# Two-layer trunk on one core: mem and its factors ahead of the memory keys, a stage between store and broadcast of the gate sums

## The chip, the core and the metric

The kernel runs on one core of a Trainium2 chip. The core has a matrix engine (TensorE, PE in the profile; its weight loads are PEld), a vector engine (VectorE, DVE), a scalar engine for activations (ScalarE, ACT), a general engine (GpSimd, POOL) and an engine that here only issues transfers (SyncE, SP). Each engine works through its own instructions; semaphores hold an instruction until its operands are there. The metric is the device time of one execution in microseconds. Before the change it is 629.26 us, the median of three runs (628.68 to 629.43).

## The reference

A trunk of two layers over 256 tokens of width 1024. Each layer has 12 self-attention heads (layer 0 with forget gates, layer 1 block-sparse with ALiBi) and 4 heads that attend to 256 fixed memory tokens, then a SwiGLU FFN. What the change touches is the memory path and the gates of layer 0:

```python
xn = rms_norm(h, norm_mix[i])
mn = rms_norm(mem, norm_mem[i])
mkv = mn @ w_mem_kv[i]                        # keys and values of the memory heads
...
log_f = jax.nn.log_sigmoid(f_logit + b_fgate[j])
F = jnp.cumsum(log_f, axis=-1)                # the gate sums
s = q @ k * scale + F[t] - F[s]               # causal, then softmax, then times v
mem_out = memory_attention(qm, mk, mv)        # softmax(qm mk / 8) mv
h = h + heads @ w_out[i]
h = h + (silu(gate) * up) @ w_down[i]
```

rms_norm divides a row by the root of its mean square. The kernel multiplies by the gain first and puts the factor per token (1 / root) in after the matmul.

## The kernel before

**Matmuls in three passes.** Every f32 operand is split in two rounded parts, hi and lo, and a product is three matmuls: hi by hi, lo by hi, hi by lo (`prod`). The split of a weight block of 128 x 1024 is one ACT instruction (hi, L204) and one DVE instruction (lo, L205).

**The weight stream.** All weights and the transposed inputs lie in one stream in the order of use, in units of up to 128 x 2048. SP loads unit after unit into `raw`, which has 4 buffers; a load waits until its buffer has been read. `weights(i, kk)` asks for a block; it splits up to 5 halves ahead (AHEAD) and loads 3 units ahead of the split (FETCH). Units that are not weights (xT, memT, mem) are only read raw. In the orders below `raw8` is unit 8 of the stream, `hi9_0` the first half of unit 9 after its split.

**What sets the order.** PE and SP keep the order in which the program is written; ACT, DVE and POOL get theirs from a scheduler when the kernel is built. On the chip every engine keeps its order.

**Layer 0 around the change.** PE computes values and gates (`v_ps`), then queries and keys of heads 0 to 3 (`qk_ps`, 96 matmuls), spreads the factors of x over the partitions (`rsb_ps_x`: a matmul with the identity; ACT copies it to `rsb_x`), and then runs `memory_heads`. That takes `mem_kv(0)` in stages: memT is multiplied with its gain and split (`split_x` into `xh_mem` and `xl_mem`, one ACT and one DVE instruction per 128 rows of memT, k = 0 to 7), and four stages of 24 matmuls give `mk_ps` and `mv_ps`, two of them from each of the two weight units (mkv). Between the stages `step()` advances the generators in `active`. Then come 48 matmuls for the memory queries (`qm_ps`), the scores of the first memory heads (`s_m`) among the 96 matmuls of heads 4 to 7, and so on.

**The factors of mem.** mem itself (not transposed) is loaded as a unit of its own; `factor` takes for each half of its tokens the mean square on ACT (`junk_mem`, L232), adds EPS on DVE (`me_mem`, L243) and takes the power -0.5 on POOL (`rs_mem`, L245). `spread` turns both `rs_mem` on PE (`rsb_ps_mem`), and ACT copies that to `rsb_mem`. The keys are multiplied with `rsb_mem` on DVE and split on ACT, DVE and POOL (`mk`, L358 to L361); the queries are split as `xqm` (L351, L353). Both must be there for `s_m`.

**The gate sums.** `gate_sums` is a generator in `active`. Its second step sums the gates on PE (`F_ps`), copies them (`fr`, DVE), stores them to memory (`fd`, L479), loads them back as a broadcast in three parts (`fk`, L482) and computes `Fq_ps` and `fq`. `bias` reads `fk` and `fq` for heads 0 and 1 at the scores after the first `s_m`.

Of the kernel before, what the change touches and what calls it, by code (L numbers as in the profile page):

```python
# [30 lines left out]
S = 256  # L31
NT = S // P
KD = D // P
# [45 lines left out]
class Plan:  # L79


    def __init__(self, a):
        self.shapes, self.blocks, self.U = [], [], {}
        U = self.U
        xT = np.ascontiguousarray(a["x"][0].T)
        memT = np.ascontiguousarray(a["mem"][0].T)
        U["xT"] = self.unit([xT], 0, KD, 0, S)
        for i in range(2):
            w = a["w_in_fox"][0] if i == 0 else a["w_in_moba"][0]
            nv = SW + (H if i == 0 else 0)  # L90
            U["vf", i] = []
            for u in range(4):
                U["vf", i].append(self.unit([w], 2 * u, 2, 2 * SW, nv))
            for g in range(3):
                if g == MEM_AT[i]:
                    if i == 0:
                        U["memT", 0] = self.unit([memT], 0, KD, 0, S)
                        self.mkv(a, 0)
                        self.blocks.append(a["mem"][0].reshape(NT, P, D).transpose(1, 0, 2).reshape(-1))
                        self.shapes.append((NT, 1, D))  # L100
                        U["mem"] = len(self.shapes) - 1
                    U["qm", i] = self.unit([w], 0, KD, 2 * SW + nv, MW)
                U["qk", i, g] = [self.unit([w[:, :SW], w[:, SW:]], 4 * u, 4, g * 2 * P, 2 * P) for u in range(2)]
            U["out", i] = [self.unit([a["w_out"][i]], 2 * j, 2, 0, D) for j in (3, 0, 1, 2)]
            U["gu", i], U["dn", i] = {}, {}
            wgu = a["w_gate_up"][i]
            for c in range(NFC + 1):
                if c < NFC:
                    U["gu", i][c] = [self.unit([wgu[:, :DFF], wgu[:, DFF:]], 4 * u, 4, c * FC, FC) for u in range(2)]
                if c > 0:  # L110
                    U["dn", i][c - 1] = self.unit([a["w_down"][i]], 2 * (c - 1), 2, 0, D)
            if i == 0:
                U["memT", 1] = self.unit([memT], 0, KD, 0, S)
                self.mkv(a, 1)
# [13 lines left out]
def trunk(ctx: ExitStack, tc: tile.TileContext, plan, stream, x, gains, norm_final, b_fgate, square, out):  # L128
# [28 lines left out]
    def bank(name):  # L157
        return Bank(pp.tile([P, 512], F32, tag="bank", name=name))
# [12 lines left out]
    U = plan.U  # L171
# [3 lines left out]
    ready, raws, counts = {}, {}, [0, 0]  # L175
    AHEAD, FETCH = 5, 3

    def fetch():
        i = counts[0]
        sh = plan.shapes[i]  # L180
        n = int(np.prod(sh))
        raw = wp.tile([P, UNIT], F32, tag="raw", name=f"raw{i}", bufs=4)
        raws[i] = raw[:, :n].rearrange("p (a b c) -> p a b c", a=sh[0], b=sh[1])
        src = stream[int(starts[i]):int(starts[i + 1])].rearrange("(p c) -> p c", p=P)
        cuts = {0: [0, n // 8, n // 4, n // 2, n], 1: [0, HEAD, n // 2, n], 2: [0, n // 2, n]}.get(i, [0, n])
        for c0, c1 in zip(cuts, cuts[1:]):
            yield lambda c0=c0, c1=c1: nc.sync.dma_start(raw[:, c0:c1], src[:, c0:c1])
        counts[0] += 1

    def fetch_to(n):  # L190
        while counts[0] < min(len(plan.shapes), n):
            for f in fetch():
                f()
# [17 lines left out]
    def weights(i, kk):  # L211

        while (i, kk) not in ready:
            split()
        while counts[1] < min(len(halves), ready[i, kk][2] + 1 + AHEAD):
            split()
        return ready[i, kk][:2]
# [11 lines left out]
    def mean_square(src, name):  # L229
        junk = ap.tile([P, D], BF16, tag="work", name=f"junk_{name}", bufs=WORK_BUFS)  # L230
        ms = sp.tile([P, 1], F32, tag="ms", name=f"ms_{name}")
        nc.scalar.activation(junk[:, :src.shape[-1]], src, AF.Square, scale=D ** -0.5, accum_out=ms)  # L232
        return ms

    def factor(src, name):

        ms = mean_square(src, name)
        return inverse_root(ms, EPS, name)

    def inverse_root(ms, more, name):  # L240

        me = sp.tile([P, 1], F32, tag="me", name=f"me_{name}")
        nc.vector.tensor_scalar_add(me, ms, more)  # L243
        rs = sp.tile([P, 1], F32, tag="rs", name=f"rs_{name}", bufs=8)
        nc.gpsimd.tensor_tensor(rs, me, minus_half, op=ALU.pow)  # L245
        return rs

    def spread(rs, name, scales, tag):

        b = bank(f"rsb_ps_{name}")  # L250
        for t in range(NT):
            b.mm(b.t[:, t * P:(t + 1) * P], rs[t].to_broadcast([P, P]), ident, stop=True)
        n = len(scales)
        r = ap.tile([P, n, S], F32, tag=f"rsb_{tag}", name=f"rsb_{name}", bufs=1)
        for j, v in enumerate(scales):
            nc.scalar.activation(r[:, j, :], b.t[:, :S], AF.Copy, scale=v)
        return r

    def xposed(name):
        xh = ap.tile([P, KD, S], F32R, tag="xh", name=f"xh_{name}", bufs=2)  # L260
        xl = ap.tile([P, KD, S], F32R, tag="xl", name=f"xl_{name}", bufs=2)
        return xh, xl
# [13 lines left out]
    def split_x(i, gain, dst, ks=range(KD)):  # L276

        fetch_to(i + 1)
        for k in ks:
            split_ps(dst[0][:, k, :], dst[1][:, k, :], raws[i][:, k, 0, :], gT[:, k, gain:gain + 1])  # L280
# [28 lines left out]
    rs_mem = []  # L309
    rsb_mem = []  # L310

    def mem_kv(i):

        xs = xposed(f"mem{i}")
        split_x(U["memT", i], 2 + i, xs, range(MEM_AHEAD))
        yield
        kb, vb = bank(f"mk_ps{i}"), bank(f"mv_ps{i}")
        for u in range(2):
            for kk in range(4):
                wh, wl = weights(U["mkv", i][u], kk)  # L320
                k = 4 * u + kk
                mv_ = (xs[0][:, k, :], xs[1][:, k, :])
                if k + MEM_AHEAD < KD:
                    split_x(U["memT", i], 2 + i, xs, (k + MEM_AHEAD,))
                for p in range(HM // 2):
                    c = slice(p * P, (p + 1) * P)
                    prod(kb, kb.t[:, p * S:(p + 1) * S], (wh[:, 0, c], wl[:, 0, c]), mv_, k == KD - 1)
                for t in range(NT):
                    c = slice(MW, 2 * MW)
                    prod(vb, vb.t[:, t * S:(t + 1) * S], tok(xs, k, t), (wh[:, 0, c], wl[:, 0, c]), k == KD - 1)  # L330
                if kk % 2:
                    yield
        if i == 0:
            fetch_to(U["mem"] + 1)
            rs_mem.extend(factor(raws[U["mem"]][:, t, 0], f"mem{t}") for t in range(NT))
            rsb_mem.append(spread(rs_mem, "mem", (1.0,), "mem")[:, 0, :])
        mk = ap.tile([P, HM // 2, S], F32, tag="work", name=f"mk{i}", bufs=WORK_BUFS)
        nc.vector.tensor_mul(mk, kb.t.rearrange("p (a s) -> p a s", a=2), rsb_mem[0].unsqueeze(1).to_broadcast([P, 2, S]))
        for p in range(HM // 2):
            split_keys(mks[p], mk[:, p])  # L340
        for t in range(NT):
            nc.scalar.activation(mvs[t][:, :, 0:DH], vb.t[:, t * S:(t + 1) * S].rearrange("p (a d) -> p a d", d=DH),
                                 AF.Copy, scale=rs_mem[t])
# [86 lines left out]
    def mixer(i, xs, rs):  # L430
# [41 lines left out]
        def gate_sums():  # L472
            yield
            fb = bank("F_ps")
            fb.mm(fb.t[:H, 0:S], lf[:, 0], prefix)
            fb.mm(fb.t[:H, P:S], lf[:, 1], prefix[:, 0:P], stop=True)
            fr = ap.tile([P, 2, S], F32, tag="work", name="fr", bufs=WORK_BUFS)[:H, 0]
            nc.vector.tensor_copy(fr, fb.t[:H, :S])
            nc.sync.dma_start(fd, fr)  # L479
            for g in range(GATE_PARTS):  # L480
                hs = slice(g * (H // GATE_PARTS), (g + 1) * (H // GATE_PARTS))
                nc.sync.dma_start(fk[:, hs], fd[hs].unsqueeze(0).to_broadcast([P, H // GATE_PARTS, S]))  # L482
            gb = bank("Fq_ps")
            for t in range(NT):
                for u in range(t + 1):
                    gb.mm(gb.t[:, t * H:(t + 1) * H], prefix[:, (t - u) * P:(t - u + 1) * P], lf[:, u], stop=u == t)
            nc.scalar.activation(fq.rearrange("p t h -> p (t h)"), gb.t[:, :NT * H], AF.Copy)
# [280 lines left out]
```

## Time and profile before

| | |
|---|---|
| median of three runs | 629.26 us |
| profiled execution, its own time | 630.81 us |
| its span | 629.0 us |
| PE busy | 611.8 us (97%) |
| PEld busy | 525.6 us (84%) |
| DVE busy | 399.9 us (64%) |
| ACT busy | 363.7 us (58%) |
| POOL busy | 60.2 us (10%) |
| mean rate of the transfers | 178 GB/s |

Durations come from the profiled execution; its own time is the span and 1.8 us around it. Busy matmuls overlap one another: back to back, two 256-column matmuls start 0.12 us apart, though one takes 0.28 us from its start to its end. A number in brackets in a timeline is the time that the engine stood idle ahead of the row, and who ended it. "PEclk" or the clock column is the granted clock of TensorE, where 1.00 is 2.4 GHz and 0.50 is 1.2 GHz.

### The profile page before, as it was taken

The page shows a single profiled execution, that of the slowest core. Times are in us where ns is not written, and L with a number is a line of the kernel's source. Part 1 is how long each engine was busy: PE and PEld are TensorE (multiplying, and loading weights), DVE is VectorE, ACT ScalarE, POOL GpSimd, SP SyncE. Part 2 cuts the span into 40 slices and gives each one's busy share as a digit, 9 for nine tenths or more (in the row PEclk, how much of TensorE's full clock was granted, in tenths as well). Part 3 has the DMA queues.
Part 4 walks back from the last instruction along what each step waited for, and adds up shares of the span by engine and source line. Part 5 has one row for each costly group of instructions (what it writes and reads, how often), then busy time and mean ns, then how long its engine had stood idle before and what let it go on. Part 6 is the DMA issues. An engine that isn't in the chain of part 4 may idle for free.

```text
span 629.0 us, 8916 instructions
## 1 busy us (share of the span) xinstructions
PE 611.8 (97%) x3364; PEld 525.6 (84%) x3364; DVE 399.9 (64%) x697; ACT 363.7 (58%) x646; POOL 60.2 (10%) x90
## 2 busy tenths in 40 slices
PE   7999899999999999999999999999999999999995
PEld 5999887778888888888899999877888888888884
DVE  4588899976455544457475589986644455445535
ACT  6679878666444444446376589876644444444423
POOL 2021344300000000000011033100000000000000
PEclk8999899999999999999999999999999999999999
DMA  8984822435554445545555533332455445555301
GB/s 289 367 315 166 338 74 103 151 143 201 202 196 168 178 194 201 179 173 207 193 185 198 216 144 114 133 135 83 160 193 200 178 172 190 198 200 198 136 2 67
DMA packets 17635, 112.27 MB, mean 178 GB/s; under 512 B 2220, under 2 KB 2744, under 8 KB 5432
## 3 DMA queue, kind: packets, MB, share of 16 engines
q1 hardware_dynamic: 17304, 111.42, 48.4%
q8 instruction: 26, 0.43, 0.3%
q10 hardware_dynamic: 288, 0.29, 0.1%
q14 instruction: 17, 0.14, 0.1%
HBM read 110.64 MB, written 1.06 MB: 178 GB/s over the span
## 4 chain that ended last, share of the span: by engine, by line
PE 84%; DVE 6%; ACT 5%; DMA 2%; issue 2%; POOL 0%; SPq 0%; POOLq 0%; ACTq 0%; DVEq 0%
PE gu L167 38%; PE d_acc L167 18%; PE qk_ps L167 9%; PE v_ps L167 6%; PE o_acc L167 5%; DMA raw<-in_stream 2%; DVE lo L205 2%; PE hT L628 2%; PE s_s L167 1%; ACT hi L204 1%; PE mv_ps L167 1%; PE qm_ps L167 1%; PE mk_ps L167 1%; ACT p_s L395 1%; PE s_m L167 1%
## 5 line engine op out<-in xcount | busy, mean ns | idle before, releaser
L205 DVE TENSOR_TENSOR lo<-raw,hi 128x1024 fp32r<-128x1024 f32 (+3 forms) x201 | 238.3, 1203 | 160.9 <-ACT hi L204 155.6
L204 ACT ACTIVATE hi<-raw 128x1024 fp32r<-128x1024 f32 (+3 forms) x201 | 204.8, 1037 | 166.4 <-PE gu L167 78.9
L167 PE MATMUL gu<-hi,xh_ffn 128*128 128x512 f32 x352 | 139.0, 395 | 0.0
L167 PE MATMUL gu<-lo,xh_ffn 128*128 128x512 f32 x352 | 137.3, 390 | 0.0
L167 PE MATMUL gu<-hi,xl_ffn 128*128 128x512 f32 x352 | 137.1, 390 | 0.0
L167 PE MATMUL d_acc<-hi,h 128*128 128x512 f32 x348 | 107.4, 390 | 0.0
L167 PEld LDWEIGHTS gu<-lo,xh_ffn 128*128 128x128 f32 x352 | 66.1, 188 | 13.9
L167 PEld LDWEIGHTS gu<-hi,xl_ffn 128*128 128x128 f32 x352 | 66.2, 188 | 13.1
L167 PEld LDWEIGHTS gu<-hi,xh_ffn 128*128 128x128 f32 x352 | 66.1, 188 | 13.0
L167 PEld LDWEIGHTS d_acc<-hi,h 128*128 128x128 f32 x348 | 65.2, 188 | 13.8 <-DVE h L224 0.4
L167 PE MATMUL d_acc<-lo,h 128*128 128x512 f32 x174 | 67.7, 389 | 0.0
L167 PE MATMUL qk_ps<-xh_x,hi 128*128 128x256 f32 x192 | 55.6, 289 | 0.0
L167 PE MATMUL qk_ps<-xh_x,lo 128*128 128x256 f32 x192 | 55.0, 287 | 0.0
L167 PE MATMUL qk_ps<-xl_x,hi 128*128 128x256 f32 x192 | 55.0, 286 | 0.0
L619 ACT ACTIVATE sg<-gu,rs_f 128x256 f32<-128x256 f32 x44 | 20.5, 466 | 40.0 <-PE gu L167 40.0
L167 PEld LDWEIGHTS d_acc<-lo,h 128*128 128x128 f32 x174 | 32.7, 188 | 6.7
L167 PEld LDWEIGHTS qk_ps<-xh_x,hi 128*128 128x128 f32 x192 | 37.5, 195 | 0.8 <-issue 0.8
L167 PEld LDWEIGHTS qk_ps<-xl_x,hi 128*128 128x128 f32 x192 | 37.6, 196 | 0.0
L167 PEld LDWEIGHTS qk_ps<-xh_x,lo 128*128 128x128 f32 x192 | 37.5, 195 | 0.0
L620 DVE TENSOR_TENSOR hh<-gu,sg 128x256 f32<-128x256 f32 x44 | 18.5, 421 | 27.0 <-ACT sg L619 27.0
L395 ACT ACTIVATE p_s<-p_s,nmax_s 128x128 f32<-128x128 f32 (+1 forms) x48 | 21.4, 446 | 11.7 <-DVE nmax_s L385 11.5
L303 POOL MEMSET xk<- 64x256 f32 x24 | 7.4, 310 | 205.0 <-DVE xl_mem L227 159.3
(160 smaller groups left out, 851.4 us busy)
## 6 DMA issues: line engine op xcount, KB each, us to landing
raw<-in_stream SPq DMA_DIRECT2D x95, 1024.0 KB, 4.8
raw<-in_stream SPq DMA_DIRECT2D x4, 768.0 KB, 4.3
raw<-in_stream SPq DMA_DIRECT2D x2, 780.0 KB, 9.0
fk<-fd SPq DMA_DIRECT2D x3, 512.0 KB, 4.8
raw<-in_stream SPq DMA_DIRECT2D x3, 390.0 KB, 6.0
h<-in_x SPq DMA_DIRECT2D x2, 512.0 KB, 8.9
raw<-in_stream SPq DMA_DIRECT2D x1, 512.0 KB, 7.8
gfin<-in_norm_final SPq DMA_DIRECT2D x1, 512.0 KB, 3.5
```

The lines of the kernel that those rows point to most:

```text
L167: nc.tensor.matmul(o, lhsT, rhs, start=self.fresh, stop=stop, skip_group_check=True)
L204: nc.scalar.activation(hi[:, c0:c1], src[:, c0:c1], AF.Copy)
L205: nc.vector.tensor_sub(lo[:, c0:c1], src[:, c0:c1], hi[:, c0:c1].bitcast(F32))
L303: nc.gpsimd.memset(dst[HOME[1 - a], a, S:].bitcast(F32), 0.0)
L395: nc.scalar.activation(pr[:, a, c], src, AF.Exp, bias=nmax[:, a, j], scale=scale, accum_out=total[:, a, j])
L619: nc.scalar.activation(sg[:, t], b[t].t[:, :FC], AF.Silu, scale=rs[t])
L620: nc.vector.tensor_mul(hh[:, t], b[t].t[:, FC:], sg[:, t])
L628: nc.tensor.transpose(b.t[:, j * S + t * P:j * S + (t + 1) * P], hh[:, t, j * P:(j + 1) * P], ident)
```

## The change

Three edits, all in layer 0. In the stream, mem's unit moves from behind the two mkv units to the place ahead of memT (it is unit 7 now and was unit 10; memT goes from 7 to 8, mkv from 8 and 9 to 9 and 10). In `mem_kv(0)`, the load of mem and the two `factor` calls move to the beginning, and `spread` moves from the end to the place between the first and the second mkv unit. In `gate_sums`, a `yield` stands between the store of the sums and their broadcast, so that the broadcast and `Fq_ps` are written one step later.

```diff
--- before.py
+++ after.py
@@ -94,11 +94,11 @@
             for g in range(3):
                 if g == MEM_AT[i]:
                     if i == 0:
-                        U["memT", 0] = self.unit([memT], 0, KD, 0, S)
-                        self.mkv(a, 0)
                         self.blocks.append(a["mem"][0].reshape(NT, P, D).transpose(1, 0, 2).reshape(-1))
                         self.shapes.append((NT, 1, D))
                         U["mem"] = len(self.shapes) - 1
+                        U["memT", 0] = self.unit([memT], 0, KD, 0, S)
+                        self.mkv(a, 0)
                     U["qm", i] = self.unit([w], 0, KD, 2 * SW + nv, MW)
                 U["qk", i, g] = [self.unit([w[:, :SW], w[:, SW:]], 4 * u, 4, g * 2 * P, 2 * P) for u in range(2)]
             U["out", i] = [self.unit([a["w_out"][i]], 2 * j, 2, 0, D) for j in (3, 0, 1, 2)]
@@ -312,6 +312,9 @@
     def mem_kv(i):
 
         xs = xposed(f"mem{i}")
+        if i == 0:
+            fetch_to(U["mem"] + 1)
+            rs_mem.extend(factor(raws[U["mem"]][:, t, 0], f"mem{t}") for t in range(NT))
         split_x(U["memT", i], 2 + i, xs, range(MEM_AHEAD))
         yield
         kb, vb = bank(f"mk_ps{i}"), bank(f"mv_ps{i}")
@@ -330,10 +333,8 @@
                     prod(vb, vb.t[:, t * S:(t + 1) * S], tok(xs, k, t), (wh[:, 0, c], wl[:, 0, c]), k == KD - 1)
                 if kk % 2:
                     yield
-        if i == 0:
-            fetch_to(U["mem"] + 1)
-            rs_mem.extend(factor(raws[U["mem"]][:, t, 0], f"mem{t}") for t in range(NT))
-            rsb_mem.append(spread(rs_mem, "mem", (1.0,), "mem")[:, 0, :])
+            if i == u == 0:
+                rsb_mem.append(spread(rs_mem, "mem", (1.0,), "mem")[:, 0, :])
         mk = ap.tile([P, HM // 2, S], F32, tag="work", name=f"mk{i}", bufs=WORK_BUFS)
         nc.vector.tensor_mul(mk, kb.t.rearrange("p (a s) -> p a s", a=2), rsb_mem[0].unsqueeze(1).to_broadcast([P, 2, S]))
         for p in range(HM // 2):
@@ -477,6 +478,7 @@
             fr = ap.tile([P, 2, S], F32, tag="work", name="fr", bufs=WORK_BUFS)[:H, 0]
             nc.vector.tensor_copy(fr, fb.t[:H, :S])
             nc.sync.dma_start(fd, fr)
+            yield
             for g in range(GATE_PARTS):
                 hs = slice(g * (H // GATE_PARTS), (g + 1) * (H // GATE_PARTS))
                 nc.sync.dma_start(fk[:, hs], fd[hs].unsqueeze(0).to_broadcast([P, H // GATE_PARTS, S]))
```

**PE, the end of the first mkv unit.** Before, the gate sums are followed by `Fq_ps` and the second mkv unit (`hi_0_375`):

```order
L167 MATMUL mv_ps_510<-hi_2_345,xl_mem_502 128x256
L167 MATMUL mv_ps_510<-lo_2_346,xh_mem_501 128x256
L167 MATMUL F_ps<-sq,lf 12x256
L167 MATMUL F_ps<-sq,lf 12x128
L167 MATMUL Fq_ps<-lf,sq 128x12 x3
L167 MATMUL mk_ps_509<-xh_mem_501,hi_0_375 128x256
L167 MATMUL mk_ps_509<-xh_mem_501,lo_0_376 128x256
```

and `rsb_ps_mem` stands behind the memory queries (`hi_4_511` is the last half of their weights), ahead of the next `qk_ps`:

```order
L167 MATMUL qm_ps_651<-xh_x_127,lo_4_512 128x256
L167 MATMUL qm_ps_651<-xl_x_128,hi_4_511 128x256
L167 MATMUL rsb_ps_mem<-sq,rs_mem_715 128x128
L167 MATMUL rsb_ps_mem<-sq,rs_mem_722 128x128
L167 MATMUL qk_ps_757<-xh_x_127,hi_0_545 128x256
```

Now it stands right behind `F_ps`, ahead of the second mkv unit (`hi_0_377`):

```order
L167 MATMUL mv_ps_524<-hi_2_347,xl_mem_502 128x256
L167 MATMUL mv_ps_524<-lo_2_348,xh_mem_501 128x256
L167 MATMUL F_ps<-sq,lf 12x256
L167 MATMUL F_ps<-sq,lf 12x128
L167 MATMUL rsb_ps_mem<-sq,rs_mem_508 128x128
L167 MATMUL rsb_ps_mem<-sq,rs_mem_515 128x128
L167 MATMUL mk_ps_523<-xh_mem_501,hi_0_377 128x256
```

The two `rsb_ps_mem` moved up by 97 rows of this list, past 48 matmuls of mkv and 48 of the queries (and past `Fq_ps`), and `Fq_ps` went 24 matmuls of mkv further back. All other PE work of the layer keeps its place.

**ACT, around `rsb_x`.** The difference; - is before, + is now (`xh_mem0` is memT, `hi8` and `hi9` the first mkv unit before and now, `xq00` the queries of heads 0 and 1):

```order
-L226 ACTIVATE xh_mem0_501<-raw7_189,gT_72 128x256 x8
-L204 ACTIVATE hi8_0_309<-raw8_223 128x1024
-L204 ACTIVATE hi8_2_345<-raw8_223 128x1024
+L226 ACTIVATE xh_mem0_501<-raw8_223,gT_72 128x256 x6
 L256 ACTIVATE rsb_x0_466<-rsb_ps_x0_463 128x256 x2
-L204 ACTIVATE hi9_0_375<-raw9_257 128x1024
-L204 ACTIVATE hi9_2_403<-raw9_257 128x1024
-L351 ACTIVATE xq00_471<-qk00_469 64x256 x2
-L358 ACTIVATE xk00_472<-qk00_469 64x256
+L226 ACTIVATE xh_mem0_501<-raw8_223,gT_72 128x256
+L204 ACTIVATE hi9_0_311<-raw9_257 128x1024
+L204 ACTIVATE hi9_2_347<-raw9_257 128x1024
```

Before, both halves of the first mkv unit are split ahead of `rsb_x`; now they stand behind it, and behind one more `xh_mem`.

**ACT, the mean squares of mem.** Before (`hi11` are weights of the memory queries, `xk01` keys of heads 2 and 3, `hi12` weights of heads 4 to 7):

```order
L204 ACTIVATE hi11_0_435<-raw11_307 128x1024
L204 ACTIVATE hi11_4_511<-raw11_307 128x1024
L487 ACTIVATE fq_340<-Fq_ps_586 128x24
L232 ACTIVATE junk_mem0_710,ms_mem0_711<-raw10_305 128x1024
L204 ACTIVATE hi12_0_545<-raw12_373 128x1024
L204 ACTIVATE hi12_2_591<-raw12_373 128x1024
L232 ACTIVATE junk_mem1_717,ms_mem1_718<-raw10_305 128x1024
```

Now:

```order
L204 ACTIVATE hi10_2_405<-raw10_305 128x1024
L359 ACTIVATE xk00_472<-qk00_469 64x256
L360 ACTIVATE xk00_472<-qk00_469 64x256
L352 ACTIVATE xq01_487<-qk01_485 64x256 x2
L359 ACTIVATE xk01_488<-qk01_485 64x256
L360 ACTIVATE xk01_488<-qk01_485 64x256
L359 ACTIVATE xk01_488<-qk01_485 64x256
L360 ACTIVATE xk01_488<-qk01_485 64x256
L232 ACTIVATE junk_mem0_503,ms_mem0_504<-raw7_189 128x1024
L204 ACTIVATE hi11_0_435<-raw11_307 128x1024
L232 ACTIVATE junk_mem1_510,ms_mem1_511<-raw7_189 128x1024
L204 ACTIVATE hi11_4_525<-raw11_307 128x1024
```

The mean squares stand right behind `xk01` and with one `hi` between them; the last instruction of memT, the eighth `xh_mem`, comes behind them. On SP the order of kinds is as it was: units 0 to 15, the store `fd`, the three `fk` directly behind it, the next unit.

## Rows read from the trace of the kernel before

**Rows 1.** The page, busy time by engine.

```profile
PE 611.8 (97%) x3364; PEld 525.6 (84%) x3364; DVE 399.9 (64%) x697; ACT 363.7 (58%) x646; POOL 60.2 (10%) x90
```

**Rows 2.** Windows by stage: us, then busy time (x instructions) per engine, clock, DMA share, GB/s.

```profile
60.00:65.00 5.00, 3.83 (x32) 3.62 (x31) 4.16 (x7) 4.82 (x11) 2.29 (x3) 1.00 0.72 265
...
77.00:92.00 15.00, 14.28 (x118) 12.70 (x117) 14.28 (x36) 12.74 (x29) 7.88 (x8) 1.00 0.20 71
...
92.00:113.00 21.00, 19.65 (x126) 15.86 (x126) 20.56 (x64) 16.09 (x42) 8.67 (x11) 1.00 0.28 101
...
113.00:134.00 21.00, 20.48 (x117) 15.97 (x116) 18.74 (x49) 12.44 (x33) 5.15 (x5) 1.00 0.42 151
```

**Rows 3.** The chain of waits, layer 0: start us, us, what.

```profile
54.01 5.85 DMA raw<-in_stream
...
64.94 0.73 POOL xqm L353
...
66.92 4.37 PE qk_ps L167 x24
...
73.19 2.88 PE qk_ps L167 x24
```

**Rows 4.** Timeline of PE: start us, us, engine, line, work, [idle before <- releaser].

```profile
38.15 0.60 PE L167 MATMUL rsb_ps_x<-sq,rs_x 128*128 128x128 f32 x4
...
38.51 0.36 PE L167 MATMUL mk_ps<-xh_mem,hi 128*128 128x256 f32 x1
...
44.43 0.82 PE L167 MATMUL F_ps<-sq,lf 128*12 128x256 f32 x4
...
45.18 0.84 PE L167 MATMUL Fq_ps<-lf,sq 128*128 128x12 f32 x6
...
57.48 0.60 PE L167 MATMUL rsb_ps_mem<-sq,rs_mem 128*128 128x128 f32 x4
...
57.84 0.36 PE L167 MATMUL qk_ps<-xh_x,hi 128*128 128x256 f32 x1
...
63.55 0.28 PE L167 MATMUL qk_ps<-xl_x,hi 128*128 128x256 f32 x1
...
65.71 1.21 PE L167 MATMUL s_m<-mk,xqm 128*128 128x256 f32 x8 [1.88 <-POOL xqm L353]
```

**Rows 5.** Windows of 1 us after the wait; columns as in Rows 2.

```profile
67.00:68.00 1.00, 1.00 (x7) 1.00 (x6) 1.00 (x4) 0.98 (x2) 0.00 (x0) 0.50 1.04 434
```

**Rows 6.** Timeline of ACT.

```profile
31.34 3.29 ACT L226 ACTIVATE xh_mem<-raw,gT 128x256 fp32r<-128x256 f32 x8
...
38.79 0.66 ACT L256 ACTIVATE rsb_x<-rsb_ps_x 128x256 f32<-128x256 f32 x2 [2.26 <-PE rsb_ps_x L167]
...
39.34 2.01 ACT L204 ACTIVATE hi<-raw 128x1024 fp32r<-128x1024 f32 x2
...
41.23 0.85 ACT L351 ACTIVATE xq<-qk 64x256 fp32r<-64x256 f32 x2
...
49.91 1.05 ACT L232 ACTIVATE junk_mem<-raw 128x1024 bf16<-128x1024 f32 x1
```

**Rows 7.** Timeline of DVE.

```profile
40.43 2.36 DVE L205 TENSOR_TENSOR lo<-raw,hi 128x1024 fp32r<-128x1024 f32 x2 [0.25 <-ACT hi L204]
...
54.31 0.15 DVE L243 TENSOR_SCALAR me_mem<-ms_mem 128x1 f32<-128x1 f32 x1
...
69.84 0.47 DVE L499 SCALAR_TENSOR_TENSOR fk<-fk,fq,sq 128x256 f32<-128x256 f32 x1
```

**Rows 8.** Timeline of POOL.

```profile
54.54 0.55 POOL L245 TENSOR_TENSOR rs_mem<-me_mem,minus_half 128x1 f32<-128x1 f32 x1 [2.40 <-DVE me_mem L243]
```

**Rows 9.** Loads issued in 24:25 us: tensors, queue, count, KB, us to landing.

```profile
raw<-in_stream SPq DMA_DIRECT2D x1, 1024.0 KB, 11.2
```

**Rows 10.** DMA issues of the page, the commonest.

```profile
raw<-in_stream SPq DMA_DIRECT2D x95, 1024.0 KB, 4.8
```

**Rows 11.** Waits of the SP queue: who waited for whom, us in total, times, longest.

```profile
SPq L482 <- DMA fd<-fr: 5.2, 1, 5.2
```

## The prediction

> **What bounds the kernel now.** I read the page's busy times first: PE works in 97% of the span [rows 1], so time is lost or won where PE stands still or runs slowly, and the windows by stage show where that is. In layer 0, PE misses 1.17 us of 60 to 65, and about 0.7, 1.35 and 0.5 us of the three stretches up to 134 [rows 2]. The first of these is one wait, continued into the next stretch: the last `qk_ps` of the piece starts at 63.55, one start is 0.12 us, so PE could go on at 63.67; `s_m` starts at 65.71 [rows 4]. That is 2.04 us late. The chain of waits gives the reason: a load from 54.01 to 59.86, then ACT's splits of keys and queries, and the POOL half of `xqm` at 64.94 [rows 3]. The loss has a second part. After the wait the granted clock is 0.50 [rows 5], so 1.2 instead of 2.4 GHz, and the next 24 `qk_ps` take 4.37 us, where 24 others take 2.88 [rows 3]: 1.49 us more. This place costs 3.53 us today.
>
> **Part 1: the first mkv unit.** Before, its two halves are split ahead of `rsb_x`, and PE starts `mk_ps` at 38.51, right behind `rsb_ps_x` [rows 4]. Now they stand behind `rsb_x` and one `xh_mem` on ACT. `rsb_x` can't start before 38.79, since it waits for PE, and lasts 0.66; ACT waits 2.26 us for it [rows 6]. The weights themselves are no problem: unit 9 was issued at 24 to 25 and landed 11.2 us later, at about 35.6 [rows 9]; the order alone holds them. So: the next ACT work starts at 39.34 as it does now; one `xh_mem`, 3.29 / 8 = 0.41; hi from 39.75 to 40.80 (1.06 for one, 1.89 from the start of two to the next instruction, 39.34 to 41.23) [rows 6]; lo on DVE, 2.36 for two, 1.2 for one [rows 7], to 42.05. The first matmul needs hi alone, the second lo, so the second starts at 42.1 instead of 38.7: PE is 3.4 us late.
>
> **Part 2: the factors.** `rsb_ps_mem` now stands on PE directly behind `F_ps`, where `Fq_ps` stood, at 45.18 in the old time [rows 4]. It needs `rs_mem` of both token halves. On ACT, from hi at 39.75: two hi 1.89; four of `xq00` and `xk00`, 0.43 each from a pair in 0.85, 1.74 [rows 6]; two hi 1.89; the other eight of the 64x256 kind 3.48; the first mean square 1.04, one hi 0.95, the second mean square 1.14 with its read-out. That ends at 51.9. On DVE, `me_mem` stands behind the lo of that hi, which ends at 52.1; 0.15 for `me_mem` [rows 7]; a hand-over of 0.08 and 0.55 on POOL [rows 8]: 52.9. PE starts `rsb_ps_mem` at 52.95, 7.77 us later than it could without any wait. This contains the 3.4 us of part 1, and a slow clock after part 1 vanishes in it. For that ACT sequence unit 11 must have landed at 49.8; its buffer is free at 43.2 (lo of unit 9), and a load takes 4.8 us at the median [rows 10]; 1.8 us are left.
>
> Could PE do the next 48 mkv matmuls instead of standing still? The row says no: at 63.67 to 65.71 PE stood idle though the 24 `qk_ps` behind `s_m` were only queued behind it. The Trainium skill (TensorE: Matmul & The Clock Gate, Step-by-step: what each phase is for) speaks of a reorder window of 64 instructions, but limits it to weight loads; matmuls stay in program order. If the window held for matmuls too, these 48 (5.8 us) would fill the second wait, and the sum would lose up to 4.4 us; by the page's limit, as by the row, it loses nothing.
>
> **Part 3: from there to `s_m`.** The rest is the same work: `Fq_ps` to the end of the queries 57.48 - 45.18 = 12.30, `rsb_ps_mem` 0.36, half of `qk_ps` 63.67 - 57.84 = 5.83 [rows 4], together 18.49, which gives 71.44. After waits of some 2 and 3 us I expect the slow clock again; I take the 1.49 us of the only wait of this size in this part, with 0 and twice that as bounds. `s_m` starts at 72.93. Are its operands there? The queries end at 67.1 on PE; ACT then has one hi waiting for exactly that, then four `xqm` (1.7), POOL 0.7 to 1.6: about 70.9. So today's wait of 2.04 us is gone, and its slow clock with it, with some 2 us in hand; were that cover used up, the wait would come back with its 1.49.
>
> The `yield` moves `fk` by one step of the program, but on SP it still stands directly behind `fd`, and nothing is loaded between. The wait for `fd`, 5.2 us [rows 11], stays. Unit 15, ahead of both, now waits for the last `xl_mem`, at about 54.7 (it was issued at 54.01), so `fk` lands some 1 us later than today, at 65 to 67; DVE asks for it after `xqm`, at 70 or later. `Fq_ps` comes 24 matmuls later on PE, and ACT waits for its copy `fq` for about 1.4 us; the 2 us in hand hide it. I take both at nothing (bounds 0 and 2).
>
> **The sum to `s_m` and its clock:** 7.77 - 2.04 = 5.73 later; the slow clock counts once before and once after. (By start times: 72.93 - 65.71 - 1.49.) Behind it the same PE work follows. DVE works 14.28 of 15 and 20.56 of 21 us there [rows 2], so the waits of PE are partly DVE's. Now one lo (1.2), one `fk` (0.47) [rows 7] and half an `xqm` are done before `s_m` that today lie behind it: some 2.1 us of lead against a PE that is 1.49 quicker. Bounds of what PE regains are 0 and its whole idle time there, 0.72 + 1.35 + 0.52 = 2.59 [rows 2]. I take 0.4, near the small end, since PE and DVE are nearly equal. That leaves +5.3: 630.81 + 5.3 = 636.1 on the profiled execution's own time. That one was 1.55 us above the median of the runs, so I forecast 629.26 + 5.3 = **634.6 us**, slower by 0.8%.
>
> **The rivals.**
> 1. *The clock stays low longer after the second wait*, for twice today's loss: +1.49 more, with no lead of DVE regained +7.2, 636.5. For it: the second wait (about 3 us, or 4.4 if the first costs no clock) is longer than today's. Against it: the only such row is the shorter one.
> 2. *No slow clock behind the second wait*: -1.49, +3.8, 633.1. For it: waits below 1 us in the later stretches leave the clock at 1.00 [rows 2]. Against it: 1.88 us of idle time did bring it down.
> 3. *The attention behind `s_m` is DVE's, and gives PE all its idle time back*: 5.73 - 2.59 = +3.1, 632.4. Against it: part of those waits are chains over three engines, which a lead of 2 us doesn't remove.
> 4. *The change does what it says*: the factors are there when PE asks at 45.18, only the wait of part 1 stays at 3.4, and today's 3.53 go: 629.1, no slower. It needs both mean squares to end on ACT by about 44. For it: ACT stands idle for 2.26 us ahead of `rsb_x` [rows 6], room for both, and mem is now the earlier load. Against it: in the order they stand behind twelve `xq` and `xk` and four hi, 9 us of work, and every timeline of ACT here runs in that order. If part 1 cost nothing either, it would be 629.26 - 3.53 = 625.7, faster.
>
> **How the numbers follow.** Chances: the forecast 0.50; rival 1 0.17; rival 2 0.13; rival 3 0.11; rival 4 0.09, of which 0.05 for 629.1 and 0.04 for 625.7. A measurement of this kernel tells about 0.2%, 1.26 us, from no change. So faster 0.04, same 0.05, slower 0.91. The range: ACT's sum of part 2 may be off by 0.7 either way (hand-overs); rival 1 with that gives 637.2 above; below, rival 3 gives 632.4, and with ACT 0.7 earlier 631.7. I take 631.8 to 637.3, which leaves rival 4 and the tails of rival 3 and rival 1 out.
>
> **What would show it.** In the profile after: a wait of PE at `mk_ps` from 38.75 to about 42, ended by ACT hi and DVE lo; a wait at `rsb_ps_mem` for POOL `rs_mem` that ends at 52.5 to 53.5; clock windows of 0.50 behind one or both; no wait at the first `s_m`, which starts near 73; `fk` still issued directly after `fd` has landed. The FFN and layer 1 should keep their lengths. If PE reaches `rsb_ps_mem` and finds `rs_mem` ready, or starts `mk_ps` at 38.5, the forecast is wrong.

## The result, and the profile after

The changed kernel takes 634.74 us, the median of four runs (633.74 to 634.97), beside 628.97 us of the kernel before, timed together with it (median of four as well): a ratio of 1.0085, 95% interval 1.0069 to 1.0101. A ratio here is the record's own estimate and need not be the quotient of the two medians, which would be 1.0092. The forecast was 634.6 us.

| | before | after |
|---|---|---|
| profiled execution, its own time | 630.81 us | 633.74 us |
| `rsb_ps_x` to the second `mk_ps` matmul | 0.56 us | 3.95 us |
| `rsb_ps_x` to the first `s_m` | 27.56 us | 33.14 us |
| first `s_m` to the first `gu` of the FFN | 68.10 us | 66.57 us |
| first `gu` to the end of the span | 495.19 us | 495.28 us |

The loss lies in layer 0, between `rsb_ps_x` and `s_m`: 5.58 us. From `s_m` to `gu` the profile of after is 1.53 us shorter, since no slow clock follows `s_m` there; the FFN and layer 1 keep their length. The profiled execution of after is the fastest of its four and that of before slower than all of its timed ones, so the profiles differ by 2.93 us and the medians by 5.77; what separates them is in the last section. Two kernels below had one execution of 2156 us among their twelve, at a recorded clock of 1.000 and unexplained; the ratios leave it out, and the medians with it lie at most 0.09 us higher.

The page's busy time by engine, after, against [rows 1]: the work of PE is the same, and what changes is where it waits.

```profile
PE 611.9 (97%) x3364; PEld 525.1 (83%) x3364; DVE 400.8 (63%) x697; ACT 364.2 (58%) x646; POOL 60.2 (10%) x90
```

Timeline of PE, after, against [rows 4]; the brackets are the idle time ahead of the row and who ended it:

```profile
39.70 0.38 PE L167 MATMUL mk_ps<-xh_mem,hi 128*128 128x256 f32 x1 [2.09 <-ACT hi L204]
40.96 0.58 PE L167 MATMUL mk_ps<-xh_mem,lo 128*128 128x256 f32 x1 [0.88 <-DVE lo L205]
...
48.27 0.82 PE L167 MATMUL F_ps<-sq,lf 128*12 128x256 f32 x4
49.88 0.49 PE L167 MATMUL rsb_ps_mem<-sq,rs_mem 128*128 128x128 f32 x2 [0.78 <-POOL rs_mem L245]
51.89 0.49 PE L167 MATMUL rsb_ps_mem<-sq,rs_mem 128*128 128x128 f32 x2 [1.53 <-POOL rs_mem L245]
52.13 0.36 PE L167 MATMUL mk_ps<-xh_mem,hi 128*128 128x256 f32 x1
...
70.15 0.40 PE L167 MATMUL s_m<-mk,xqm 128*128 128x256 f32 x2
```

Two waits are new: the first mkv unit (hi, then lo), and the two halves of the factors. The 1.88 us at `s_m` are gone: the row has no bracket.

Timeline of ACT, after, against [rows 6]:

```profile
37.65 0.66 ACT L256 ACTIVATE rsb_x<-rsb_ps_x 128x256 f32<-128x256 f32 x2 [2.88 <-PE rsb_ps_x L167]
38.20 0.51 ACT L226 ACTIVATE xh_mem<-raw,gT 128x256 fp32r<-128x256 f32 x1
38.59 2.00 ACT L204 ACTIVATE hi<-raw 128x1024 fp32r<-128x1024 f32 x2
...
47.79 1.06 ACT L232 ACTIVATE junk_mem<-raw 128x1024 bf16<-128x1024 f32 x1
...
49.79 1.04 ACT L232 ACTIVATE junk_mem<-raw 128x1024 bf16<-128x1024 f32 x1
...
51.78 0.50 ACT L226 ACTIVATE xh_mem<-raw,gT 128x256 fp32r<-128x256 f32 x1
```

ACT stands idle for 2.88 us with the weights of the first mkv unit landed (at 34.70), since `rsb_x` is ahead of them, and gets to the mean squares of mem 9 us after the hi that PE waited for. The POOL rows that release PE answer to [rows 8]:

```profile
49.27 0.55 POOL L245 TENSOR_TENSOR rs_mem<-me_mem,minus_half 128x1 f32<-128x1 f32 x1 [1.90 <-DVE me_mem L243]
51.29 0.55 POOL L245 TENSOR_TENSOR rs_mem<-me_mem,minus_half 128x1 f32<-128x1 f32 x1 [1.46 <-DVE me_mem L243]
```

Windows of 1 us, after (the columns are us, busy time and instructions of PE, PEld, DVE, ACT, POOL, clock, DMA share, GB/s), against [rows 5]: behind the first wait the clock is 0.50, behind the second and at `s_m` it is 1.00.

```profile
41.00:42.00 1.00, 1.00 (x5) 1.00 (x6) 1.00 (x1) 0.95 (x3) 0.96 (x1) 0.50 0.00 0
...
52.00:53.00 1.00, 1.00 (x9) 1.00 (x10) 1.00 (x1) 1.00 (x2) 0.00 (x0) 1.00 0.42 147
70.00:71.00 1.00, 1.00 (x11) 1.00 (x10) 1.00 (x4) 1.00 (x1) 0.00 (x0) 1.00 0.97 410
```

SP, after: the store, and the broadcast directly behind its landing, as in the order before.

```profile
54.01 0.44 SPq L480 DMA_DIRECT2D fd<-fr  x1
60.94 1.82 SPq L484 DMA_DIRECT2D fk<-fd  x3
```

### The profile page after: what moved, and what is told of

Same layout as the page of the kernel before. It is cut to its first block, busy times and chain, and to the rows that moved or that the text cites. A ratio compares the mean times of both kernels' runs of the same rounds, so it can differ in the third digit from the quotient of the medians.

```text
span 632.0 us, 8915 instructions
## 1 busy us (share of the span) xinstructions
PE 611.9 (97%) x3364; PEld 525.1 (83%) x3364; DVE 400.8 (63%) x697; ACT 364.2 (58%) x646; POOL 60.2 (10%) x90
## 4 chain that ended last, share of the span: by engine, by line
PE 85%; DVE 7%; ACT 4%; issue 1%; DMA 1%; SPq 0%; POOL 0%; POOLq 0%; DVEq 0%
PE gu L167 38%; PE d_acc L167 18%; PE qk_ps L167 8%; PE v_ps L167 5%; PE o_acc L167 5%; PE qm_ps L167 2%; DVE lo L205 2%; PE hT L630 2%; PE mk_ps L167 1%; PE mv_ps L167 1%; ACT hi L204 1%; PE s_s L167 1%; PE o_s L167 1%; DMA raw<-in_stream 1%; DVE p_s L386 1%
```

## The experiments

Each is timed against the kernel before, in three groups. Its medians were 629.36 us for the first four experiments below, 628.25 for the yield alone (first time), the move alone, both causes taken away and the memory heads, and 629.33 for the yield alone (second time) and the last kernel without the yield. The middle group ran on another chip than the other two, so times of different groups are compared by their ratios. A ratio has its 95% interval.

**The changed kernel a second time.** No edit.

> The changed kernel itself, once more, for a second profile and more times. Theory: about 634.7 us against 629 of the kernel before (+5.3 to +5.9). In its first profile the clock stayed at 1.00 behind the second wait (rsb_ps_mem) and also at the start, while the profile of the kernel before had a slow stretch of 3.4 us at the start. If the slow stretches come and go between executions of one kernel, this profile differs in their number: PE counts 1.5 us more for each, and the granted clock of an execution goes with it (0.994 in the first profile, 0.989 to 0.991 in the other three executions). Rival: the clock is the same each time, so a second profile shows again one slow stretch alone, behind the first wait, and then +5.8 in the medians against +4.1 between the profiles (once both are counted from rsb_ps_x) must have another reason.

Measured: 634.45 us, 1.0085 [1.0064, 1.0105]. The waits of PE are the same to 0.01 us, but here the clock also falls behind the second, as the timeline of PE and a window show:

```profile
48.80 0.49 PE L167 MATMUL rsb_ps_mem<-sq,rs_mem 128*128 128x128 f32 x2 [0.77 <-POOL rs_mem L245]
50.81 0.58 PE L167 MATMUL rsb_ps_mem<-sq,rs_mem 128*128 128x128 f32 x1 [1.53 <-POOL rs_mem L245]
...
70.31 0.28 PE L167 MATMUL s_m<-mk,xqm 128*128 128x256 f32 x1
```

```profile
52.00:53.00 1.00, 1.00 (x7) 1.00 (x6) 1.00 (x3) 1.00 (x3) 0.00 (x0) 0.50 1.05 442
```

From `rsb_ps_mem`'s second half to the memory queries are 7.98 us here (50.81 to 58.79) and 6.74 in the first profile (51.89 to 58.63): 1.24 us for this slow stretch. Whether it comes differs from execution to execution of one kernel.

**The spread back behind both mkv units.** It keeps the wait of part 1 and takes that of part 2 away.

```diff
-            if i == u == 0:
-                rsb_mem.append(spread(rs_mem, "mem", (1.0,), "mem")[:, 0, :])
+        if i == 0:
+            rsb_mem.append(spread(rs_mem, "mem", (1.0,), "mem")[:, 0, :])
```

> The changed kernel with the spread of the factors back behind both mkv units; mem and its factors stay ahead. Theory (two waits, one from the hi of the first mkv unit behind rsb_x, one from rsb_ps_mem behind F_ps): the second wait is gone, the first stays with 3.4 us and a slow stretch of 1.5 behind it, s_m starts near 68.6 without a wait, so +3.4 + 1.5 - 2.0 - 1.5 = +1.4: 630.4 (629.5 to 631.5). Rival (what costs is that mem holds a buffer of the stream for longer, so that the loads come late): the spread's place changes nothing, 634.7.

Measured: 631.64 us, 1.0042 [1.0026, 1.0058], a little above the expected range. Its timeline of PE:

```profile
40.22 0.39 PE L167 MATMUL mk_ps<-xh_mem,lo 128*128 128x256 f32 x1 [0.88 <-DVE lo L205]
...
60.56 0.49 PE L167 MATMUL rsb_ps_mem<-sq,rs_mem 128*128 128x128 f32 x3
...
67.25 0.51 PE L167 MATMUL s_m<-mk,xqm 128*128 128x256 f32 x2 [0.33 <-POOL xqm L354]
```

PE asks for the factors at 60.56 and they are there. So the place of the spread makes about half of the loss. What its removal gives is less than the 4.4 us between the two waits of the prediction, since the slow clock behind part 1 no longer vanishes in a second wait: the 7.32 us from 40.22 to `F_ps` at 47.54 were 5.72 before [rows 4].

**mem between the two mkv units in the stream.** The spread stays early; the first mkv unit is split as early as in the kernel before.

```diff
+                        U["memT", 0] = self.unit([memT], 0, KD, 0, S)
+                        U["mkv", 0] = [self.unit([a["w_mem_kv"][0]], 0, 4, 0, 2 * MW)]
                         self.blocks.append(a["mem"][0].reshape(NT, P, D).transpose(1, 0, 2).reshape(-1))
                         self.shapes.append((NT, 1, D))
                         U["mem"] = len(self.shapes) - 1
-                        U["memT", 0] = self.unit([memT], 0, KD, 0, S)
-                        self.mkv(a, 0)
+                        U["mkv", 0].append(self.unit([a["w_mem_kv"][0]], 4, 4, 0, 2 * MW))
```

> The changed kernel with the stream in the order memT, first mkv unit, mem, second mkv unit; factors and spread stay where the change put them. Both hi of the first mkv unit then stand ahead of rsb_x on ACT as before the change, and the mean squares behind xk01 and one hi. Theory: mk_ps starts at 38.5 without a wait; ACT's work from xq00 at 40.2 is 12 x 0.435 + 1.89 + 0.95 + 1.04 + 1.14 = 10.2, so the second rs_mem is there at 51.3 and PE waits 6.1 us at rsb_ps_mem; minus the 2.0 of today's s_m: +4.1 with a slow stretch behind it, +2.6 without: 633.1 (631.5 to 634). Rival (the wait of the first mkv unit is the whole cost): 629 or less.

Measured: 633.82 us, 1.0078 [1.0059, 1.0098]. Its timeline of PE:

```profile
36.45 0.60 PE L168 MATMUL rsb_ps_x<-sq,rs_x 128*128 128x128 f32 x4
36.81 0.36 PE L168 MATMUL mk_ps<-xh_mem,hi 128*128 128x256 f32 x1
...
48.78 0.80 PE L168 MATMUL rsb_ps_mem<-sq,rs_mem 128*128 128x128 f32 x2 [5.23 <-POOL rs_mem L246]
...
109.28 0.71 PE L168 MATMUL s_s<-xk,xq 128*128 128x256 f32 x4 [2.30 <-POOL xk L363]
```

The wait of part 1 is gone, and up to `s_m` the loss is nearly the same (5.21 us in this profile, 5.58 and 6.81 in those of the changed kernel): PE waits 5.23 us at `rsb_ps_mem` instead, less than the 6.1 I expected. The second wait is set by ACT's sequence up to the mean squares (they run at 46.62 and 47.66 here), whatever PE did ahead of it. Not all of this kernel's loss is that wait: from `s_m` to `gu` it takes 68.34 us, 1.77 more than after, with the wait of 2.30 us at `s_s` and a clock of 0.50 behind it. Why `xk` comes late there is not shown.

**The factors of mem left out**, replaced by a constant 1.0; the rest as changed.

```diff
-            rs_mem.extend(factor(raws[U["mem"]][:, t, 0], f"mem{t}") for t in range(NT))
+            for t in range(NT):
+                one = cp.tile([P, 1], F32, name=f"one{t}")
+                nc.gpsimd.memset(one, 1.0)
+                rs_mem.append(one)
```

> The changed kernel without the factors of mem: the mean squares, me_mem and the powers of layer 0's and 1's memory path are left out, and a constant 1.0 stands in their place; mem is still loaded. Nothing is left for PE to wait for at rsb_ps_mem, and ACT has 2.2 us less to do. Theory: the second wait is gone, the first stays: +1.4 as in the run with the late spread, 630.4 (629.0 to 631.0). Rival (PE's order itself or the late loads cost the time): 633 or more.

Measured: 630.64 us, 1.0025 [1.0013, 1.0037], as expected. Its timeline of PE:

```profile
40.47 0.58 PE L167 MATMUL mk_ps<-xh_mem,lo 128*128 128x256 f32 x1 [0.88 <-DVE lo L205]
...
48.38 0.38 PE L167 MATMUL rsb_ps_mem<-sq,one 128*128 128x128 f32 x1
```

With the factors at hand PE does not stop at `rsb_ps_mem`, and most of the loss is gone. It is their lateness that costs, not the place of the two matmuls on PE; what is left is part 1 with its slow clock. (ACT is also relieved of the two mean squares here, so the share of each part is not exact.)

**The yield alone, twice.** The kernel before with the third edit only.

```diff
             nc.sync.dma_start(fd, fr)
+            yield
```

> The kernel before with the yield between fd and fk alone. On PE, Fq_ps comes 24 matmuls later and ACT copies fq after two more hi; on SP fk still stands directly behind fd. Theory: nothing waits for fq or fk in this stretch (bias is asked for near 64 us), so no difference: 629.4 (628.4 to 630.4). Rival (the yield carries part of the cost of the change, by ACT standing still for Fq_ps): 630.8 or more.

> The kernel before with the yield alone, a second time. In the first profile the load behind which ACT splits the keys landed 0.28 us later in the span than before, the wait at s_m was 2.36 us instead of 1.88, and the median was 0.29% above the kernel before. Theory A: the yield itself does nothing to that load; what differed is how many executions of each kernel had slow stretches of the clock, and a second look gives a ratio whose interval holds 1 or comes near it (0.999 to 1.002). Theory B: the yield costs 0.2 to 0.4% again, 1.002 to 1.004, and the wait at s_m is longer than 2.1 us again.

Measured: 630.96 us, 1.0029 [1.0016, 1.0043], which I had not expected; the second time 629.74 us, 1.0015 [1.0001, 1.0028]. In the two profiles `s_m` waits 2.36 and 2.07 us. The timelines of ACT and of PE in the first, and that of PE in the second:

```profile
60.23 1.06 ACT L204 ACTIVATE hi<-raw 128x1024 fp32r<-128x1024 f32 x1 [1.62 <-DMA raw<-in_stream]
```

```profile
65.99 0.39 PE L167 MATMUL s_m<-mk,xqm 128*128 128x256 f32 x1 [2.36 <-POOL xqm L353]
```

```profile
65.92 0.38 PE L167 MATMUL s_m<-mk,xqm 128*128 128x256 f32 x1 [2.07 <-POOL xqm L353]
```

That is 0.48 and 0.19 us more than in the kernel before [rows 4], by a load that landed 0.46 and 0.16 us later, counted from `rsb_ps_x`. From `rsb_ps_x` to the first `gu` the two profiles take 96.11 and 95.78 us, before 95.66. So the edit's own place shows 0.45 and 0.12 us of the 1.8 and 0.9 us that the ratios say. The rest may be a matter of how often the slow stretches of the clock come (last section): of the kernel before 15 of 29 and 7 of 23 executions in these two groups took 628.30 us or less, of the yield alone none of 11 and one of 12. Why the load lands later with the yield isn't settled.

**The move of mem alone**, the changed kernel without the yield.

> The changed kernel without the yield. Fq_ps stands ahead of rsb_ps_mem again, so PE has 0.7 us more to do before it waits for rs_mem, and the end of that wait is set by ACT as before. Theory: the same as the changed kernel, 634.5 (633.5 to 635.3). Rival (the yield is what costs): 629.4.

Measured: 636.14 us, 1.0102 [1.0081, 1.0122], above the expected range. The waits of part 1 and part 2 are there with 2.09, 0.88 and 1.53 us, and both had a slow stretch behind them in the profile. The interval meets that of the changed kernel: the whole loss is the move's, and with it the yield costs nothing that shows.

**Both causes taken away, the factors still early**: the stream of the third experiment with the spread of the second.

> The changed kernel with both causes taken away: the stream in the order memT, first mkv unit, mem, second mkv unit, and the spread back behind both mkv units. The factors are still computed earlier than before the change. Theory: mk_ps starts right behind rsb_ps_x, rsb_ps_mem finds rs_mem ready, and the wait at s_m stays, since ACT's split of the keys still ends its queue of work there, as before: 629.2 (628.2 to 630.5). Rival A (factors ahead of the keys do help once nothing waits for them too early): 626 or less. Rival B (a third cost of the change is left, by the loads): 631 or more.

Measured: 626.86 us, 0.9969 [0.9957, 0.9981]: faster than both kernels, about 2.3 us below what I expected and above the 626 of rival A. Its PE, its ACT and a window behind `s_m`:

```profile
36.21 0.60 PE L168 MATMUL rsb_ps_x<-sq,rs_x 128*128 128x128 f32 x4
36.57 0.36 PE L168 MATMUL mk_ps<-xh_mem,hi 128*128 128x256 f32 x1
...
44.16 0.39 PE L168 MATMUL mk_ps<-xh_mem,lo 128*128 128x256 f32 x1 [0.53 <-DVE lo L206]
...
63.05 0.50 PE L168 MATMUL s_m<-mk,xqm 128*128 128x256 f32 x2 [0.39 <-POOL xqm L355]
```

```profile
56.95 0.38 ACT L257 ACTIVATE rsb_mem<-rsb_ps_mem 128x256 f32<-128x256 f32 x1 [0.95 <-PE rsb_ps_mem L168]
57.24 1.05 ACT L205 ACTIVATE hi<-raw 128x1024 fp32r<-128x1024 f32 x1
```

```profile
64.00:65.00 1.00, 1.00 (x11) 1.00 (x10) 0.97 (x4) 0.98 (x2) 0.00 (x0) 1.00 0.99 410
```

The row that explains it is the `hi` at 57.24, the last work of ACT ahead of the splits of the keys. Before, it waits for a load issued at 54.01 [rows 3], and that load goes into mem's buffer, which the second mean square has read only just before (the kernel before, timeline of ACT):

```profile
53.79 0.19 ACT L232 ACTIVATION_READ_ACCUMULATOR junk_mem<-raw 128x1 f32 x1
...
59.95 1.06 ACT L204 ACTIVATE hi<-raw 128x1024 fp32r<-128x1024 f32 x1 [1.18 <-DMA raw<-in_stream]
```

The read-out ends at 53.98, and the load is issued 0.03 us later. (The profile names ACT's next instruction, `mv`, as what released the load; but `mv` ends at 54.34, after the issue.) With mem read earlier another buffer is free for this load, freed by a `lo` of DVE that ends at 50.78, as SP shows:

```profile
50.80 0.33 SPq L188 DMA_DIRECT2D raw<-in_stream  x1
```

The `hi` no longer waits for a transfer (its own landed at 56.97, 0.27 us ahead of it); what ACT waits for just before is the late spread. The times of the two profiles can't be subtracted as they stand, since `rsb_ps_x` starts 1.94 us earlier here. Counted from `rsb_ps_x`, the load is issued 14.59 us on instead of 15.86, the `hi` starts 0.77 us earlier and `s_m` 0.72 us earlier. `s_m` waits 0.39 instead of 1.88 us and no slow clock follows, which is the larger part of the difference of these two profiles: up to `gu` this one takes 93.43 us, before 95.66. No run moves the reading of mem alone; that it is the cause rests on these rows and on the next run, which repeats them.

**The same without the yield.**

> As the kernel with mem between the two weight units, its factors taken early and their spread left at the old place, but without the yield between the store of the gate sums and their broadcast. Theory A: that kernel's gain (0.31%, 626.86 us) comes from the load that ACT waits for ahead of the splits of the keys: it is issued at 50.8 instead of 54.0, since the buffer it needs is free earlier, so that the wait of PE at the first s_m is 0.39 us instead of 1.88 and no slow clock follows it; the yield has no part in it. Then this kernel takes the same time, 626.3 to 627.5 us, with a wait under 0.6 us at s_m. Theory B: the yield costs the 0.3% that it cost by itself, and costs them here too: then this kernel is about 625 us, faster than with the yield by more than 1 us. Theory C: the yield is needed, since the broadcast blocks SP otherwise: 628 us or more, a wait over 1.5 us at s_m.

Measured: 627.00 us, 0.9970 [0.9957, 0.9984]: the same time. The gain doesn't need the yield. Its timeline of PE:

```profile
63.37 0.50 PE L168 MATMUL s_m<-mk,xqm 128*128 128x256 f32 x2 [1.03 <-POOL xqm L355]
```

The wait is 1.03 us here, longer than the 0.6 that I had named, and the time is the same; no window of 0.50 stands behind it. The bracket is longer because PE gets there earlier, mostly by the 0.53 us at `mk_ps` that it does not wait here: counted from `rsb_ps_x`, `s_m` starts after 26.83 us, with the yield after 26.84. (The load of theory A is issued 1.3 us earlier than before by that count; 50.8 against 54.0 holds the earlier start of the whole profile too.) From `rsb_ps_x` to `gu` it takes 93.44 us, with the yield 93.43.

**The memory heads one step later** in the kernel before, to cover the wait at `s_m` with other work of PE.

```diff
-IDLE_MEM = (1, 1)
+IDLE_MEM = (2, 1)
```

> The kernel before with the memory heads of layer 0 starting one step later (first number of IDLE_MEM 2 in place of 1): 24 matmuls of qk_ps stand ahead of the first s_m. Theory: xqm is ready near 65.7, PE comes to s_m near 66.7 and doesn't wait: -2.0, and the slow stretch of 1.5 that followed in some executions is gone; on the median -2.8: 626.6 (625.4 to 627.8). Rival (the softmax of the memory heads comes later by as much, and a wait at pT_m or behind takes the place): 629 or more.

Measured: 629.48 us, 1.0011 [0.9997, 1.0025]: no difference; the rival held. Its timeline of PE, and a window behind the last of these waits:

```profile
65.42 0.40 PE L167 MATMUL s_m<-mk,xqm 128*128 128x256 f32 x2
...
75.04 1.18 PE L406 MATMUL pT_m<-sq,p_m 128*128 128x128 f32 x8 [0.76 <-DVE nmax_s L385]
80.64 0.30 PE L406 MATMUL pT_m<-sq,p_m 128*128 128x128 f32 x1 [0.90 <-DVE p_m L399]
81.36 0.55 PE L406 MATMUL pT_m<-sq,p_m 128*128 128x128 f32 x3 [0.42 <-DVE p_m L399]
82.36 0.72 PE L406 MATMUL pT_m<-sq,p_m 128*128 128x128 f32 x4 [0.45 <-DVE p_m L399]
```

```profile
84.00:85.00 1.00, 1.00 (x7) 1.00 (x7) 1.00 (x2) 0.94 (x3) 0.82 (x1) 0.50 0.01 0
```

The wait at `s_m` is gone and four waits for DVE stand where its work came too late, with the slow clock behind them. In these two kernels the same wait pays when the data come earlier, and not when PE's order is changed around it.

## Why the prediction was right, step by step

| step | predicted | measured |
|---|---|---|
| part 1: the second `mk_ps` matmul late by | 3.4 us | 3.39 us |
| part 2: second `rsb_ps_mem` after `rsb_ps_x` | 14.80 us | 14.88 and 14.87 us |
| slow clock behind the second wait | 1.49 us | 0 in one profile, 1.24 in the other |
| wait at `s_m` | gone | gone |
| PE regains behind `s_m` | 0.4 us | 0.04 us |
| `s_m` later, and less the slow clock of before | 7.22, 5.73 us | 5.58, 4.09 and 6.81, 5.32 us |
| the time | 634.6 us | 634.74 us |

**Part 1 and part 2** came out of the order of ACT and the durations of its rows, to within 0.1 us. The two terms were not added but taken as one ACT sequence, and the third experiment shows that this was the point: without the first wait the second grows to 5.23 us. One margin was smaller than the sum had it: the load of unit 11 landed at 48.04, 0.8 us ahead of its split on ACT, where I had 1.8 in hand. Putting the spread back halves the loss (1.0042 of 1.0085), and leaving the factors out takes two thirds of it (1.0025).

**The first slow clock** did vanish in the second wait: PE lost about 1.6 us from 40.96 to 48.27 and stood still at `rsb_ps_mem` all the same. In the kernel with the late spread, which has no second wait, it counts.

**PE did not work past the waiting matmul.** It stood idle for 0.78 and 1.53 us with the mkv matmuls queued behind `rsb_ps_mem`, the first 36 of them with their operands there: the split of their weights ended at 45.90. The last 12 needed the eighth `xh_mem`, which ACT made only at 51.78, so the 48 of the prediction were 36. That PE waited all the same agrees with the Trainium skill (TensorE: Matmul & The Clock Gate, Step-by-step: what each phase is for), which has matmuls stay in program order.

**The slow clock behind the second wait** was one size for what varies: the first profile is rival 2 (no slow clock), the second has 1.24 us of it. Rival 1, a clock that stays low for longer, shows in neither. How many of the four timed runs had the slow stretch isn't shown, but each has its granted clock on record: 0.994 for the profiled one, 0.989 to 0.991 for the other three, so those had more of slow clock than the first profile shows.

**The regained time** was mis-sized, 0.04 for 0.4 us: from `s_m` to `gu` the kernel before takes 68.10 - 1.49 = 66.61 us without its slow clock, after 66.57. The second profile takes 66.59. The lead of DVE bought nothing, so rival 3 fell. Rival 4 fell with the wait at `rsb_ps_mem`.

**The last 0.14 us are luck.** In the second profile `s_m` comes 5.32 us later where the sum had 5.73, and PE regains 0.02 where the sum had 0.4: the two errors cancel. The forecast also started from 629.26 us, and the kernel before measured beside it was 628.97; the increase was forecast as 5.3 us, and is 5.77 by the medians and 5.3 by the ratio.

**The yield**, taken at nothing with bounds 0 and 2 us, stays within them: 1.8 and 0.9 us by itself in the kernel before, nothing that shows with the move or in the fastest kernel. `fk` was issued directly behind `fd`'s landing as predicted, and no wait in the trace names it. It landed later than I had it: its three parts at 66.14, 67.36 and 69.46, which counted from `rsb_ps_x` is 3.2 to 3.9 us later than before instead of 1. DVE asked for it at 69.90, so this cost nothing.

**What the prediction did not see**: the load that sets the wait at `s_m` was waiting for mem's buffer. I read that load off the chain [rows 3] as given. Had I asked what freed its buffer, the useful half of this change (reading mem earlier) could have shown, and with it the version at 626.86 us.

## What to carry to other kernels

Moving work ahead of an engine's queue moves everything queued behind it: find the instruction on ACT or DVE that the moved consumer will wait for, and add up the engine's rows in their new order up to it, one sum for several waits in a row. When a chain begins with a load, ask which read freed its buffer; an early read of a rarely used tensor can be worth more than early arithmetic on it (in the kernel before `rsb_ps_mem` stood without a wait already [rows 4], so early factors alone had nothing to give). And put the consumer on PE only where its operand is ready: here the same early factors cost 0.85% with an early spread behind a late weight split, and gave 0.3% without these two.

## What the runs showed of the hardware

**One kernel's executions differ by slow stretches of TensorE's clock.** 71 runs of the kernel before lie from 627.09 to 631.29 us: 24 up to 628.30, 37 from 628.62 to 630.15, 10 from 630.29 up. Their recorded clock sorts them nearly as well: all of the 24 have 0.997 or 0.998, and 43 of the other 47 have 0.993 to 0.996. Against those 24 (median 627.84 us) the two kernels at 626.86 and 627.00 are still 0.8 to 1.0 us faster; the rest of their gain would then be fewer slow stretches. One stretch that comes and goes is at the start, in code that all these kernels share. From the `v_ps` matmul behind its wait for the first weights to `rsb_ps_x` the profile of before takes 30.04 us, those of the yield alone 30.04 and 30.09, those of the changed kernel and of the later memory heads 28.49 and 28.51. The 1.5 us are slow matmuls in the first microseconds: from 9 to 11 us the profile of before has 7 matmuls at a clock of 0.50. In the second profile of the yield alone the clock column does not show it, but the count of PE's instructions in the same window does; it is x8 (the first fence), and x13 with the later memory heads (the second fence):

```profile
9.00:11.00 2.00, 2.00 (x8) 2.00 (x7) 2.00 (x3) 1.61 (x3) 0.00 (x0) 1.00 1.05 415
```

```profile
9.00:11.00 2.00, 2.00 (x13) 2.00 (x12) 2.00 (x4) 1.97 (x4) 0.00 (x0) 1.00 1.06 436
```

This can account for the two profiles differing by 2.84 us less than the medians: the one of before has the stretch at the start (1.55 us) and the one behind `s_m`, the one of after lacks the one at the start and the one behind its second wait (1.24 us). Which of them the timed executions had was not profiled, and why a stretch comes in one execution and not in the next stays open.

**Waits and the clock.** Waits of 1.88, 2.07 and 2.36 us at `s_m` were followed by a clock of 0.50 in their profiles; so were the 2.09 and 0.88 us at `mk_ps` in all five profiles that have them, and the 2.30 us at `s_s` in the kernel with mem between the mkv units. Waits of 0.33, 0.39 and 1.03 us at `s_m` were not. The 0.78 and 1.53 us, with one half of the spread between them, were in one profile and not in another of the same kernel. In the wait of 5.23 us the clock fell while PE stood still: it was 0.50 from 46 us on, and still from 51 to 52, 2.2 us after PE had gone on:

```profile
51.00:52.00 1.00, 1.00 (x7) 1.00 (x7) 1.00 (x1) 1.00 (x2) 0.00 (x0) 0.50 1.01 426
```
